# Attention scores from half-array products: three per map, two maps in the two halves of the array's rows

## The chip, the cores and the metric

The kernel runs on one core of a Trainium2 chip. The metric is the time of one execution on the device in microseconds (us). TensorE (PE in the profile) multiplies matrices, VectorE (DVE), ScalarE (ACT) and GpSimd (POOL) work element by element, SyncE (SP) issues the DMAs. PE loads one operand of each product into its array (the weight load, PEld) and streams the columns of the other through it.

## The reference

One encoder layer is applied to two token groups of 1024 and 256 tokens, with model width 1024. It normalises, projects, runs two kinds of attention, projects back, and goes on with an MLP and a gated embedding. What matters here are the scores:

```python
def _diff_attention(q, k, v, lam, slopes):      # mixer A: 4 heads, two softmax maps each
        sc = jnp.einsum('bqhcd,bkhcd->bhcqk', qb, k) * scale
        sc = sc - slopes[None, :, None, None, None] * dist[None, None, None]
        pr = jax.nn.softmax(sc, axis=-1)
        w = pr[:, :, 0] - lam * pr[:, :, 1]
        return jnp.einsum('bhqk,bkhe->bqhe', w, v)

def _gqa_attention(q, k, v):                    # mixer B: 8 query heads, 2 key/value heads
        sc = jnp.einsum('bqngd,bknd->bngqk', qb, k) * scale
        pr = jax.nn.softmax(sc, axis=-1)
        return jnp.einsum('bngqk,bknd->bqngd', pr, v)
```

Each score is a product over a head dimension of 64, in single precision.

## The kernel before, in words

Single precision is reached with two numbers of a shorter format (float32r): a value is split into a high part and a low part, and products of the parts are added up. The queries (`qd`) and keys (`kd`) lie in DRAM with both parts.

Work in the attention is cut into units (`plan_unit`): a block of 256 queries against its group's 1024 keys ("full"; 48 units) or 256 keys ("short"; 12 units). A unit of mixer A is one head with both maps; a unit of mixer B is one of the two heads that share a tile of queries (`c` says which), for both sub-blocks `i` of 128 queries. Each score tile `sc` is 128 queries by up to 1024 keys in PSUM, and there are two buffers of it.

For one tile, `qk` issues products over all 128 rows of the array. The tile `kt` holds the keys' high parts in rows 0 to 63 and the low parts in rows 64 to 127; the tile `qt` holds the queries' high part in both halves of the rows, and beside it the low part in both halves. Two products (high queries, low queries) thus give all four combinations, for each 512 columns:

```python
            for v in range(2):
                for h0 in range(0, sn, 512):
                    PE.matmul(ps[:, h0:h0 + n], shared["q"][:, cc, v, i * P:(i + 1) * P],
                              kt[:, s0 + h0:s0 + h0 + n], start=v == 0, stop=v == 1)
```

A full tile takes four products, a short tile two. Then VectorE reads the tile: for A it adds the distance term, takes the minimum and writes `p` (L555), for B it takes the maximum (L559), after which ScalarE reads the tile once more for the exponential (L567). When the last reader is done the buffer is free for the next tile. GpSimd or VectorE scales the result (L576 to L588), PE transposes it (`tr`, L603), ScalarE and VectorE split the transposes into high and low parts (`ph` L609, `pl` L614), and PE multiplies them with the values (`av`, L627).

These steps are put into numbered rounds: a unit's `qk` stands some rounds ahead of its transposes (`AW` for A, `BW` for B). In each round, products of the remaining projections (`psa`) and of the output projection (`pso`, both L218) are woven in from a generator, as many as `RATIO` times the costs that the parts of the round return. The rounds give the order in which instructions are written down; a scheduler then sets the final order on each engine, with an instruction placed where its operands and buffers are ready by its own reckoning. Each engine carries out its list in that final order.

Of the kernel before, what the change touches and what calls it, by code (L numbers as in the profile page):

```python
# [23 lines left out]
P = 128  # L24
# [4 lines left out]
T = NP_TOK + NS_TOK  # L29
NT = T // P  # L30
# [4 lines left out]
DISTW = 1920  # L35
# [5 lines left out]
def f(ap):  # L41
    return ap.bitcast(F32)
# [3 lines left out]
def encoder_kernel(ctx: ExitStack, tc: tile.TileContext, x, xT, pT, w_in, w_out, w_ff1, w_ff2, w_gate, w_proj,  # L46
# [3 lines left out]
    LEAD = {4: 2000., 5: 2000., 6: 2000.}  # L50
    PRE = 14000
    Y = (2,0,0)
    QM = 0
    AW = (-7, -6, -5, -4)
    BW = (-6, -4)
    AVD = 2
    PHB = 4
    PLB = 4
    PB = 6
    QTB = 3  # L60
# [17 lines left out]
    AOB = 3  # L78
    LDA = 2
    LC = 500.0  # L80
    RATIO = 0.43

    V, S, G, PE = nc.vector, nc.scalar, nc.gpsimd, nc.tensor
    ON_POOL = (0,)
    dma = nc.sync.dma_start
# [20 lines left out]
    qd = [dp.tile([2, P, T], F32, name=f"qd{i}") for i in range(8)]  # L106
    kd = [dp.tile([2, P, T], F32, name=f"kd{i}") for i in range(5)]
# [308 lines left out]
    for (c0, cn) in TCH:  # L416
        ps = pj("psr")
# [13 lines left out]
    pp = pool("pp", space=PSUM, bufs=1, stack=ats)  # L431
# [1 line left out]
    TILES = {  # L433
        "mm": ([P, 2], F32, 4), "ll": ([P, 2], F32, 4), "rl": ([P, 2], F32, 4), "rla": ([P, 2], F32, 4),
        "o": ([P, 256], F32, 3), "osq": ([P, 256], F32, 1), "or": ([P, 256], F32, 1), "pad": ([P, 16], F32, 1),
        "kt": ([P, T], F32R, 3), f"vt{P}": ([P, NT, P], F32R, 1), "ph": ([P, 2, 256], F32R, PHB), "pl": ([P, 2, 256], F32R, PLB),
        "qt": ([P, 2, 2, 256], F32R, QTB), "p": ([P, 1024], F32, PB), "dist": ([P, DISTW], F16, 1),
        f"vt{2 * P}": ([P, NT, 2 * P], F32R, 1), "pq": ([P, 256], F32, 4), "ml": ([P, 2, 256], F32R, 1),
        "snv": ([P, 256], F32, 1), "snu": ([P, 256], F32, 1),
    }  # L440
# [3 lines left out]
    def tl(tag):  # L444
        shape, dt, bufs = TILES[tag]
        return ap.tile(shape, dt, tag=tag, name=tag, bufs=bufs)
# [21 lines left out]

    def load_q(i, t0):
        qt = tl("qt")  # L470
        for dup in range(2):
            if QM:
                dma(f(qt[dup * 64:(dup + 1) * 64]), qd[i][:, :, t0:t0 + 256].rearrange("v (c d) t -> d c v t", d=64))
                continue
            for c in range(2):
                dma(f(qt[dup * 64:(dup + 1) * 64, c]),
                    qd[i][:, c * 64:(c + 1) * 64, t0:t0 + 256].rearrange("v d t -> d v t"))
        return qt

    dst_t = tl("dist")  # L480
# [1 line left out]
    kv = {}  # L482
# [3 lines left out]
    def at(r, ph, fn):  # L486
        rounds[r].append((PH[ph], len(rounds[r]), fn))
# [15 lines left out]
        at(r, "fin", hi)  # L503
        at(r + 1, "fin", lo)

    def plan_unit(kind, idx, t0, c, b, shared):

        is_a = kind == "A"
        s0, sn = SEGS[t0 >= NP_TOK]
        full = sn == NP_TOK  # L510
        nj = sn // 256
        st = {"ws": [None, None], "p": {}}
        if is_a:
            order = [(0, 0), (0, 1), (1, 0), (1, 1)]
            when = [b + q for q in AW] if full else [b - 5, b - 5, b - 4, b - 4]
        else:
            order = [(0, c), (1, c)]
            when = [b + q for q in BW] if full else [b - 4, b - 4]

        def start():  # L520
            if is_a:
                if ("A", idx) not in kv:
                    kv["A", idx] = ([load_k(idx, i) for i in range(2)],
                                    load_v(vad[idx].rearrange("t v d -> t (v d)")))
# [6 lines left out]
            if c == 0:  # L531
                shared["q"] = load_q(idx, t0)

        at(when[0] - 3, "ld", start)

        def qk(i, cc):
            ps = pp.tile([P, 1024], F32, tag="sc", name="sc", bufs=2)
            kt = st["k"][cc] if is_a else st["k"]
            for v in range(2):
                for h0 in range(0, sn, 512):  # L540
                    n = min(512, sn)
                    PE.matmul(ps[:, h0:h0 + n], shared["q"][:, cc, v, i * P:(i + 1) * P],  # L542
                              kt[:, s0 + h0:s0 + h0 + n], start=v == 0, stop=v == 1)
            st["ps", i, cc] = ps
            return sn * 0.844

        def mx(i, cc):
            ps = st["ps", i, cc]
            p = tl("p" if full else "pq")
            st["p"][i, cc] = p  # L550
            if is_a:
                if cc == 0:
                    st["m", i], st["l", i], st["r", i] = (tl(n) for n in ("mm", "ll", "rla"))
                off = DIST0 - (t0 - s0 + i * P)
                V.tensor_tensor_reduce(out=p[:, :sn], in0=ps[:, :sn], in1=dst_t[:, off:off + sn], scale=SLOPES[idx],  # L555
                                       scalar=3.0e38, op0=ALU.add, op1=ALU.min, accum_out=st["m", i][:, cc:cc + 1])
            else:
                st["m", i], st["l", i], st["r", i] = (tl(n) for n in ("mm", "ll", "rl"))
                V.tensor_reduce(out=st["m", i][:, 0:1], in_=ps[:, :sn], axis=AX.X, op=ALU.max, negate=True)  # L559

        def ex(i, cc):
            p = st["p"][i, cc]
            if is_a:
                S.activation(p[:, :sn], p[:, :sn], AF.Exp, scale=-1.0, bias=st["m", i][:, cc:cc + 1],  # L564
                             accum_out=st["l", i][:, cc:cc + 1])
            else:
                S.activation(p[:, :sn], st["ps", i, cc][:, :sn], AF.Exp, scale=1.0, bias=st["m", i][:, 0:1],  # L567
                             accum_out=st["l", i][:, 0:1])

        def cb(i):  # L570
            rl, l = st["r", i], st["l", i]
            if is_a:


                V.reciprocal(rl[:, 1:2], l[:, 1:2])
                G.tensor_scalar(rl[:, 0:1], rl[:, 1:2], l[:, 0:1], neglam, op0=ALU.mult, op1=ALU.mult)  # L576
                p = st["p"][i, 0]
                p1 = st["p"][i, 1]
                if i in ON_POOL and full:
                    G.tensor_scalar(p1[:, :sn], p1[:, :sn], rl[:, 0:1], 1.0, op0=ALU.mult, op1=ALU.mult)  # L580
# [10 lines left out]
        for (i, cc), r in zip(order, when):  # L591
            at(r, "qk", functools.partial(qk, i, cc))
            at(r + 1, "mx", functools.partial(mx, i, cc))
            at(r + 1, "ex", functools.partial(ex, i, cc))
            if not is_a or cc == 1:
                at(r + 2, "cb", functools.partial(cb, i))

        def tr(j2):
            t = pp.tile([P, 2, 256], F32, tag="tr", name="tr", bufs=2)
# [72 lines left out]
            mixed_out(e + 4, idx, t0, lambda: st["o"])  # L672
        else:
            def f1():
                if c == 0:
# [7 lines left out]
            if c == 1:  # L683
                mixed_out(e + 1, idx, t0, lambda: shared["mx"])

    b = 9
    for h in range(4):
        al = [("A", h, t0, 0, {}) for t0 in (0, 256, 1024, 512, 768)]
        bl = []
        for t0 in (0, 256, 512, 768, 1024):  # L690
            sh = {}
            bl += [("B", 4 + h, t0, c, sh) for c in range(2)]
        for kind, idx, t0, c, sh in (bl[0], bl[1], al[0], bl[8], bl[2], bl[3], al[1], bl[9], bl[4], bl[5],
                                     al[2], al[3], bl[6], bl[7], al[4]):
            plan_unit(kind, idx, t0, c, b, sh)
            b += 4 if t0 < NP_TOK else 1


# [173 lines left out]
    while owed > 0:  # L872
        d = next(side)
# [655 lines left out]
```

## Time and profile before

| | |
|---|---|
| median of 3 runs | 1742.87 us (1741.82 to 1745.6) |
| the profiled execution | 1746.48 us, of which the span of its instructions is 1744.7 us |
| PE busy | 1681.1 us, 96% of the span, 9868 products |
| VectorE, ScalarE, GpSimd busy | 67%, 49%, 38% of the span |
| the stretch with scores | 221 to 698 us from the span's start |
| score products (L542) | 576 |

A row of a group reads: line, engine, operation, tile written <- tiles read, rows and columns of the array that are used, shape, count, then busy time in us and mean length in ns, then idle time of the engine ahead of them and what ended it. A row of the timeline reads: start in us, time to the group's end in us, engine and instruction, count. Products are pipelined: the next one starts before the last one's record ends, so a price is read from start to start.

### The profile page before, as it was taken

The page shows a single profiled execution, that of the slowest core. Times are in us where ns is not written, and L with a number is a line of the kernel's source. Part 1 is how long each engine was busy: PE and PEld are TensorE (multiplying, and loading weights), DVE is VectorE, ACT ScalarE, POOL GpSimd, SP SyncE. Part 2 cuts the span into 40 slices and gives each one's busy share as a digit, 9 for nine tenths or more (in the row PEclk, how much of TensorE's full clock was granted, in tenths as well). Part 3 has the DMA queues.
Part 4 walks back from the last instruction along what each step waited for, and adds up shares of the span by engine and source line. Part 5 has one row for each costly group of instructions (what it writes and reads, how often), then busy time and mean ns, then how long its engine had stood idle before and what let it go on. Part 6 is the DMA issues. An engine that isn't in the chain of part 4 may idle for free.

```text
span 1744.7 us, 27438 instructions
## 1 busy us (share of the span) xinstructions
PE 1681.1 (96%) x9868; PEld 1500.5 (86%) x9868; DVE 1172.2 (67%) x2061; ACT 854.7 (49%) x1735; POOL 660.0 (38%) x638
## 2 busy tenths in 40 slices
PE   8899989999989999997999999999999999999997
PEld 8899878888878888777999999998888888888886
DVE  6757458878778778589766666665664865354666
ACT  7523258777767668455333333333433333344554
POOL 1224345756755556335423332320433400001442
PEclk9999999999999999998999999999999999999999
DMA  9723473443874532471533334339665366532111
GB/s 297 236 74 107 146 191 118 116 130 94 223 217 122 144 117 86 140 228 57 179 138 144 132 127 142 140 136 386 230 226 191 120 205 191 183 112 81 41 43 49
DMA packets 198520, 263.47 MB, mean 151 GB/s; under 512 B 14064, under 2 KB 132720, under 8 KB 198384
## 3 DMA queue, kind: packets, MB, share of 16 engines
q1 hardware_dynamic: 198384, 261.72, 46.9%
q8 instruction: 78, 1.28, 0.3%
q14 instruction: 58, 0.48, 0.1%
HBM read 175.16 MB, written 81.27 MB: 147 GB/s over the span
## 4 chain that ended last, share of the span: by engine, by line
PE 81%; DMA 6%; DVE 4%; issue 3%; POOL 2%; ACT 2%; SPq 1%; POOLq 0%; DVEq 0%; ACTq 0%
PE sc L542 6%; PE psa L218 5%; PE av L627 5%; PE psg L149 5%; PE pso L218 5%; PE tr L603 4%; PE psb L218 3%; PE psv L218 2%; PE psp L149 1%; DMA xt<-in_x 1%; DMA xr<-in_xT 1%; DMA vt<-vad 1%; DVE pl L614 1%; PE f__16369 L149 1%; PE f__16711 L149 1%
## 5 line engine op out<-in xcount | busy, mean ns | idle before, releaser
L614 DVE TENSOR_TENSOR pl<-tr,ph 128x512 fp32r<-128x512 f32 x204 | 138.0, 684 | 43.3 <-ACT ph L609 42.5
L1238 ACT ACTIVATE ao<-ar 128x1280 fp32r<-128x1280 f32 x56 | 71.2, 1272 | 191.0 <-PE f__16373 L149 37.9
L542 PE MATMUL sc<-kt,qt 128*128 128x512 f32 (+1 forms) x576 | 154.9, 392 | 8.2 <-issue 3.8
L1240 DVE TENSOR_TENSOR ao<-ar,ao 128x1280 fp32r<-128x1280 f32 x56 | 93.3, 1665 | 103.4 <-ACT ao L1238 103.4
L609 ACT ACTIVATE ph<-tr 128x512 fp32r<-128x512 f32 x204 | 119.8, 595 | 69.9 <-PE tr L603 68.2
L218 PE MATMUL pso<-ow,mt 128*128 128x512 f32 x480 | 121.7, 399 | 7.5 <-DMA mt<-md 5.7
L542 PEld LDWEIGHTS sc<-kt,qt 128*128 128x128 f32 x576 | 101.0, 191 | 26.9 <-issue 4.2
L603 PE MATMUL tr<-ident,p 128*128 128x128 f32 x768 | 115.6, 274 | 4.1 <-DVE pl L614 3.4
L149 PE MATMUL psg<-gw,n 128*128 128x512 f32 (+1 forms) x504 | 115.3, 385 | 0.0
L218 PEld LDWEIGHTS pso<-ow,mt 128*128 128x128 f32 x480 | 88.9, 190 | 25.4 <-DMA mt<-md 6.4
L149 PEld LDWEIGHTS psg<-gw,n 128*128 128x128 f32 x504 | 91.1, 188 | 19.4
L603 PEld LDWEIGHTS tr<-ident,p 128*128 128x128 f32 x768 | 90.5, 141 | 18.4 <-DVE pl L614 5.1
L627 PE MATMUL av<-ph,vt 128*128 128x256 f32 x544 | 102.6, 290 | 1.4 <-DVE zl L740 1.0
L559 DVE TENSOR_REDUCE mm<-sc 128x1 f32<-128x1024 f32 (+1 forms) x80 | 84.1, 1056 | 25.2 <-PE sc L542 24.5
L1027 ACT ACTIVATE w<-w1s 128x512 fp32r<-128x512 f32 x64 | 40.0, 627 | 122.3 <-POOL w1s L1034 6.8
L588 POOL TENSOR_SCALAR p<-p,rl 128x1024 f32<-128x1024 f32 x64 | 72.9, 1141 | 57.5 <-DVE rl L586 52.8
L627 PE MATMUL av<-pl,vt 128*128 128x256 f32 x408 | 93.6, 311 | 0.0
L627 PEld LDWEIGHTS av<-ph,vt 128*128 128x128 f32 x544 | 83.3, 191 | 7.3 <-DVE zl L740 1.9
L567 ACT ACTIVATE p<-sc,mm 128x1024 f32<-128x1024 f32 x64 | 71.4, 1115 | 33.7 <-DVE mm L559 26.8
L555 DVE CUSTOM_DVE_ANT_0 p<-sc,dist 128x1024 f32<-128x1024 f32 x64 | 76.9, 1217 | 5.2 <-PE sc L542 4.2
L564 ACT ACTIVATE p<-p,mm 128x1024 f32<-128x1024 f32 x64 | 73.5, 1150 | 7.7 <-DVE mm L555 7.6
L1413 POOL TENSOR_TENSOR p_l<-pr,p_h 128x256 fp32r<-128x256 f32 x10 | 7.8, 781 | 183.4 <-ACT p_h L1412 183.4
(1508 smaller groups left out, 4786.8 us busy)
## 6 DMA issues: line engine op xcount, KB each, us to landing
ar<-ad SPq DMA_DIRECT2D x56, 640.0 KB, 4.1
w2r<-in_w_ff SPq DMA_DIRECT2D x56, 512.0 KB, 4.5
qt<-qd SPq DMA_DIRECT2D x160, 128.0 KB, 3.2
ad<-q SPq DMA_DIRECT2D x64, 320.0 KB, 2.2
w1r<-in_w_ff SPq DMA_DIRECT2D x32, 512.0 KB, 3.8
ad<-qs SPq DMA_DIRECT2D x48, 320.0 KB, 2.2
md<-ml SPq DMA_DIRECT2D x40, 256.0 KB, 2.5
mt<-md SPq DMA_DIRECT2D x80, 128.0 KB, 3.4
```

The source lines that it names most:

```text
L149: PE.matmul(ps, a, b, start=start and i == 0, stop=stop and i == n - 1)
L218: PE.matmul(ps, a, b, start=i == 0, stop=i == n - 1)
L542: PE.matmul(ps[:, h0:h0 + n], shared["q"][:, cc, v, i * P:(i + 1) * P], kt[:, s0 + h0:s0 + h0 + n], start=v == 0, stop=v == 1)
L555: V.tensor_tensor_reduce(out=p[:, :sn], in0=ps[:, :sn], in1=dst_t[:, off:off + sn], scale=SLOPES[idx], scalar=3.0e38, op0=ALU.add, op1=ALU ...
L559: V.tensor_reduce(out=st["m", i][:, 0:1], in_=ps[:, :sn], axis=AX.X, op=ALU.max, negate=True)
L564: S.activation(p[:, :sn], p[:, :sn], AF.Exp, scale=-1.0, bias=st["m", i][:, cc:cc + 1], accum_out=st["l", i][:, cc:cc + 1])
L588: G.tensor_scalar(p[:, :sn], p[:, :sn], rl[:, 0:1], 1.0, op0=ALU.mult, op1=ALU.mult)
L603: PE.transpose(t[:, jj, i * P:(i + 1) * P], st["ws"][i][:, j * P:(j + 1) * P], ident)
L609: S.activation(ph, st["tr", j2], AF.Copy)
L614: V.tensor_tensor(pl, st["tr", j2], f(st["ph", j2][:]), op=ALU.subtract)
L627: PE.matmul(st["av"][:, :256], x_, y_, start=j2 == 0 and n == 0, stop=j2 == nj - 1 and n == len(pr) - 1)
L1240: V.tensor_tensor(ao[:, 1], a, f(ao[:, 0]), op=ALU.subtract)
```

## The change

The two maps of a head (A), or the two query heads that share keys (B), get their score tiles together. The keys' high parts and low parts are now two tiles, with map 0 (or the first head) in rows 0 to 63 and map 1 (or the second) in rows 64 to 127; for B, where both use the same keys, these are loaded into both halves. The query tile holds each part once. For each tile there are three products over 64 rows, high by high, high by low, low by high; the fourth, low by low, is left out. A full pair takes twelve half-array products where two full tiles took eight products on all rows; a short pair takes six where there were four. The loop writes one for the upper half of the rows and one for the lower by turns, into the two score buffers.

A unit of B is now one sub-block of 128 queries for both heads (`i0`), so its transposes and values run over heads where they ran over sub-blocks, and its output is put together in two halves (`f1`). The number of `qk` calls falls from 160 to 80. The offsets `AW` and `BW` follow from that, `RATIO` rises from 0.43 to 0.46, and there are four `kt` buffers instead of three.

```diff
-    QM = 0
-    AW = (-7, -6, -5, -4)
-    BW = (-6, -4)
+    AW = (-6, -4)
+    BW = -5
...
-    RATIO = 0.43
+    RATIO = 0.46
...
-    def load_k(i, c):
-        kt = tl("kt")
+    def load_k(i, j=None):
+
+        kts = []
         for v in range(2):
-            dma(f(kt[v * 64:(v + 1) * 64, :]), kd[i][v, c * 64:(c + 1) * 64, :])
-        return kt
+            kt = tl("kt")
+            if j is None:
+                dma(f(kt[:]), kd[i][v])
+            else:
+                for dup in range(2):
+                    dma(f(kt[dup * 64:(dup + 1) * 64, :]), kd[i][v, j * 64:(j + 1) * 64, :])
+            kts.append(kt)
+        return kts
...
     def load_q(i, t0):
         qt = tl("qt")
...
+        dma(f(qt[:]), qd[i][:, :, t0:t0 + 256].rearrange("v p t -> p v t"))
         return qt
...
-        def qk(i, cc):
-            ps = pp.tile([P, 1024], F32, tag="sc", name="sc", bufs=2)
-            kt = st["k"][cc] if is_a else st["k"]
-            for v in range(2):
-                for h0 in range(0, sn, 512):
-                    n = min(512, sn)
-                    PE.matmul(ps[:, h0:h0 + n], shared["q"][:, cc, v, i * P:(i + 1) * P],
-                              kt[:, s0 + h0:s0 + h0 + n], start=v == 0, stop=v == 1)
-            st["ps", i, cc] = ps
-            return sn * 0.844
+        def qk(i):
+
+            pss = [pp.tile([P, 1024], F32, tag="sc", name="sc", bufs=2) for _ in range(2)]
+            n = min(512, sn)
+            for h0 in range(0, sn, 512):
+                for m, (vq, vk) in enumerate(((0, 0), (0, 1), (1, 0))):
+                    for cc in range(2):
+                        rows = slice(cc * 64, cc * 64 + 64)
+                        PE.matmul(pss[cc][:, h0:h0 + n], shared["q"][rows, vq, i * P:(i + 1) * P],
+                                  st["k"][vk][rows, s0 + h0:s0 + h0 + n], start=m == 0, stop=m == 2)
+            for cc in range(2):
+                st["ps", i, cc] = pss[cc]
+            return sn * 1.266
...
-                V.reciprocal(rl[:, 0:1], l[:, 0:1])
-                p = st["p"][i, c]
-                G.tensor_scalar(p[:, :sn], p[:, :sn], rl[:, 0:1], 1.0, op0=ALU.mult, op1=ALU.mult)
+                V.reciprocal(rl, l)
+                for cc in range(2):
+                    p = st["p"][i, cc]
+                    G.tensor_scalar(p[:, :sn], p[:, :sn], rl[:, cc:cc + 1], 1.0, op0=ALU.mult, op1=ALU.mult)
+                    st["ws"][cc] = p
+                return
...
-                x_, y_ = slice(c * 64, c * 64 + 64), slice(64 - c * 64, P - c * 64)
                 tm = tl("osq")
-                S.activation(tm[x_], st["av"][y_, :256], AF.Copy)
-                V.tensor_tensor(shared["mx"][x_], st["av"][x_, :256], tm[x_], op=ALU.add)
+                for cc in range(2):
+                    x_, y_ = slice(cc * 64, cc * 64 + 64), slice(64 - cc * 64, P - cc * 64)
+                    w = slice(cc * P, cc * P + P)
+                    S.activation(tm[x_, w], st["av"][y_, w], AF.Copy)
+                    V.tensor_tensor(shared["mx"][x_, i0 * P:i0 * P + P], st["av"][x_, w], tm[x_, w], op=ALU.add)
```

The final order on PE, first near the start of the attention, before the change, where mixer A's first head gets its first scores. `sc` is a score tile, `kt` and `qt` are keys and queries, `tr` the transposes of B's unit ahead of it and `av` its value products; a count stands at a row's end. The first four score products are those of map 0, the next four those of map 1, and the last four of the eight are map 0 of the next sub-block.

```order
L542 MATMUL sc<-kt,qt 128x512 x4
L603 MATMUL tr<-ident,p 128x128 x8
L542 MATMUL sc<-kt,qt 128x512 x8
L627 MATMUL av<-ph,vt_3087 128x256 x2
L627 MATMUL av<-pl,vt_3087 128x256 x2
```

A map's four products stand together. At the same place of the changed program, the first six are those of map 0, in the upper half of the rows (`sc_3228`), and the last six those of map 1, in the lower half (`sc_3229`):

```order
L543 MATMUL sc<-kt,qt 128x512 x6
L610 MATMUL tr<-ident,p 128x128 x4
L634 MATMUL av<-pl,vt_3090 128x256 x2
L634 MATMUL av<-ph,vt_3090 128x256 x2
L610 MATMUL tr<-ident,p 128x128 x4
L634 MATMUL av<-pl,vt_3090 128x256 x2
L543 MATMUL sc<-kt,qt 128x512 x6
```

All six products of the upper half now stand together, then transposes and value products follow, and the six of the lower half come after these. With the tiles' numbers, the first of the two runs and the row ahead of it read (`kt_3164` is the tile of high keys, `kt_3166` that of low keys):

```order
L634 MATMUL av_3248<-ph_3201,vt128_3090 128x256 x2
L543 MATMUL sc_3228<-kt_3164,qt_3170 128x512
L543 MATMUL sc_3228<-kt_3166,qt_3170 128x512
L543 MATMUL sc_3228<-kt_3164,qt_3170 128x512 x2
L543 MATMUL sc_3228<-kt_3166,qt_3170 128x512
L543 MATMUL sc_3228<-kt_3164,qt_3170 128x512
```

One score tile is written in all six, over both of its blocks of 512 keys. A little earlier, at the second pair of B, the two halves stand beside each other in part (`sc_3172` upper, `sc_3173` lower):

```order
L543 MATMUL sc_3172<-kt_3084,qt_3092 128x512
L543 MATMUL sc_3172<-kt_3087,qt_3092 128x512
L543 MATMUL sc_3172<-kt_3084,qt_3092 128x512
L543 MATMUL sc_3173<-kt_3084,qt_3092 128x512
L543 MATMUL sc_3173<-kt_3087,qt_3092 128x512
L543 MATMUL sc_3173<-kt_3084,qt_3092 128x512
L543 MATMUL sc_3172<-kt_3084,qt_3092 128x512
L543 MATMUL sc_3173<-kt_3084,qt_3092 128x512
L543 MATMUL sc_3172<-kt_3087,qt_3092 128x512
L543 MATMUL sc_3173<-kt_3087,qt_3092 128x512
L543 MATMUL sc_3172<-kt_3084,qt_3092 128x512
L543 MATMUL sc_3173<-kt_3084,qt_3092 128x512
```

Three of the upper half stand ahead of three of the lower, and only the last six go by turns, as the loop writes them.

More of the change, by code (lines that the diff above doesn't have):

```diff
@@ L435, in encoder_kernel @@
         "o": ([P, 256], F32, 3), "osq": ([P, 256], F32, 1), "or": ([P, 256], F32, 1), "pad": ([P, 16], F32, 1),
-        "kt": ([P, T], F32R, 3), f"vt{P}": ([P, NT, P], F32R, 1), "ph": ([P, 2, 256], F32R, PHB), "pl": ([P, 2, 256], F32R, PLB),
-        "qt": ([P, 2, 2, 256], F32R, QTB), "p": ([P, 1024], F32, PB), "dist": ([P, DISTW], F16, 1),
+        "kt": ([P, T], F32R, 4), f"vt{P}": ([P, NT, P], F32R, 1), "ph": ([P, 2, 256], F32R, PHB), "pl": ([P, 2, 256], F32R, PLB),
+        "qt": ([P, 2, 256], F32R, QTB), "p": ([P, 1024], F32, PB), "dist": ([P, DISTW], F16, 1),
         f"vt{2 * P}": ([P, NT, 2 * P], F32R, 1), "pq": ([P, 256], F32, 4), "ml": ([P, 2, 256], F32R, 1),
@@ L470, in load_q @@
         qt = tl("qt")
[L471 to L477, printed above, removed]
+        dma(f(qt[:]), qd[i][:, :, t0:t0 + 256].rearrange("v p t -> p v t"))
         return qt
@@ L504, in mixed_out, with plan_unit @@
         at(r + 1, "fin", lo)
-    def plan_unit(kind, idx, t0, c, b, shared):
+    def plan_unit(kind, idx, t0, i0, b, shared):
         is_a = kind == "A"
@@ L513, in plan_unit @@
         if is_a:
-            order = [(0, 0), (0, 1), (1, 0), (1, 1)]
-            when = [b + q for q in AW] if full else [b - 5, b - 5, b - 4, b - 4]
-        else:
-            order = [(0, c), (1, c)]
-            when = [b + q for q in BW] if full else [b - 4, b - 4]
+            when = {i: b + q for i, q in enumerate(AW)}
+        else:
+            when = {i0: b + BW}
         def start():
@@ L522, in start @@
                 if ("A", idx) not in kv:
-                    kv["A", idx] = ([load_k(idx, i) for i in range(2)],
+                    kv["A", idx] = (load_k(idx),
                                     load_v(vad[idx].rearrange("t v d -> t (v d)")))
@@ L530, in start @@
                 st["k"], st["v"] = kv["B", j]
-            if c == 0:
+            if i0 == 0:
                 shared["q"] = load_q(idx, t0)
-        at(when[0] - 3, "ld", start)
-        def qk(i, cc):
-            ps = pp.tile([P, 1024], F32, tag="sc", name="sc", bufs=2)
-            kt = st["k"][cc] if is_a else st["k"]
-            for v in range(2):
-                for h0 in range(0, sn, 512):
-                    n = min(512, sn)
-                    PE.matmul(ps[:, h0:h0 + n], shared["q"][:, cc, v, i * P:(i + 1) * P],
-                              kt[:, s0 + h0:s0 + h0 + n], start=v == 0, stop=v == 1)
-            st["ps", i, cc] = ps
-            return sn * 0.844
+        at(min(when.values()) - 3, "ld", start)
+        def qk(i):
[10 more added lines that the diff above has]
+            return sn * 1.266
         def mx(i, cc):
@@ L557, in mx @@
             else:
-                st["m", i], st["l", i], st["r", i] = (tl(n) for n in ("mm", "ll", "rl"))
-                V.tensor_reduce(out=st["m", i][:, 0:1], in_=ps[:, :sn], axis=AX.X, op=ALU.max, negate=True)
+                if cc == 0:
+                    st["m", i], st["l", i], st["r", i] = (tl(n) for n in ("mm", "ll", "rl"))
+                V.tensor_reduce(out=st["m", i][:, cc:cc + 1], in_=ps[:, :sn], axis=AX.X, op=ALU.max, negate=True)
         def ex(i, cc):
@@ L566, in ex @@
             else:
-                S.activation(p[:, :sn], st["ps", i, cc][:, :sn], AF.Exp, scale=1.0, bias=st["m", i][:, 0:1],
-                             accum_out=st["l", i][:, 0:1])
+                S.activation(p[:, :sn], st["ps", i, cc][:, :sn], AF.Exp, scale=1.0, bias=st["m", i][:, cc:cc + 1],
+                             accum_out=st["l", i][:, cc:cc + 1])
         def cb(i):
@@ L585, in cb @@
             else:
-                V.reciprocal(rl[:, 0:1], l[:, 0:1])
-                p = st["p"][i, c]
-                G.tensor_scalar(p[:, :sn], p[:, :sn], rl[:, 0:1], 1.0, op0=ALU.mult, op1=ALU.mult)
-            st["ws"][i] = p
[L591 to L596, printed above, removed]
+                V.reciprocal(rl, l)
[4 more added lines that the diff above has]
+                return
+            st["ws"][i] = p
+        for i, r in when.items():
+            at(r, "qk", functools.partial(qk, i))
+            for cc in range(2):
+                at(r + 1, "mx", functools.partial(mx, i, cc))
+            for cc in range(2):
+                at(r + 1, "ex", functools.partial(ex, i, cc))
+            at(r + 2, "cb", functools.partial(cb, i))
         def tr(j2):
@@ L674, in f1 @@
             def f1():
-                if c == 0:
+                if i0 == 0:
                     shared["mx"] = tl("o")
-                x_, y_ = slice(c * 64, c * 64 + 64), slice(64 - c * 64, P - c * 64)
                 tm = tl("osq")
-                S.activation(tm[x_], st["av"][y_, :256], AF.Copy)
-                V.tensor_tensor(shared["mx"][x_], st["av"][x_, :256], tm[x_], op=ALU.add)
+                for cc in range(2):
+                    x_, y_ = slice(cc * 64, cc * 64 + 64), slice(64 - cc * 64, P - cc * 64)
+                    w = slice(cc * P, cc * P + P)
+                    S.activation(tm[x_, w], st["av"][y_, w], AF.Copy)
+                    V.tensor_tensor(shared["mx"][x_, i0 * P:i0 * P + P], st["av"][x_, w], tm[x_, w], op=ALU.add)
             at(e, "fin", f1)
-            if c == 1:
+            if i0 == 1:
                 mixed_out(e + 1, idx, t0, lambda: shared["mx"])
@@ L691, in encoder_kernel @@
             sh = {}
-            bl += [("B", 4 + h, t0, c, sh) for c in range(2)]
-        for kind, idx, t0, c, sh in (bl[0], bl[1], al[0], bl[8], bl[2], bl[3], al[1], bl[9], bl[4], bl[5],
+            bl += [("B", 4 + h, t0, i, sh) for i in range(2)]
+        for kind, idx, t0, i, sh in (bl[0], bl[1], al[0], bl[8], bl[2], bl[3], al[1], bl[9], bl[4], bl[5],
                                      al[2], al[3], bl[6], bl[7], al[4]):
-            plan_unit(kind, idx, t0, c, b, sh)
+            plan_unit(kind, idx, t0, i, b, sh)
             b += 4 if t0 < NP_TOK else 1
```

## The prediction

> **What bounds the kernel now.** I read the page's busy shares first, then the stretch of the attention, then the groups of TensorE there, its waits, and last its timeline.
>
> ```profile
> PE 1681.1 (96%) x9868; PEld 1500.5 (86%) x9868; DVE 1172.2 (67%) x2061; ACT 854.7 (49%) x1735; POOL 660.0 (38%) x638
> PE 81%; DMA 6%; DVE 4%; issue 3%; POOL 2%; ACT 2%; SPq 1%; POOLq 0%; DVEq 0%; ACTq 0%
> 215.00:705.00 490.00, 468.35 (x2912) 409.76 (x2911) 381.68 (x692) 348.58 (x726) 300.73 (x355) 0.99 0.49 140
> ```
>
> TensorE (PE) is busy 96% of the span and has 81% of the chain that ended last. The third row is the stretch of the attention (columns: busy time of PE, weight loads, VectorE, ScalarE, GpSimd, then granted clock, DMA share, GB/s). Of its 490 us PE works 468.35, so 21.65 us are idle, and the next engine, VectorE, is busy 78% of it. Time added to PE's queue here adds to the kernel's time, less what the 21.65 us can take up. Who owns them:
>
> ```profile
> PE av L649 <- DVE osq L644: 6.4, 3, 3.0
> PE sc L542 <- issue: 3.8, 1, 3.8
> PE tr L603 <- DVE pl L614: 2.5, 8, 0.8
> PE pso L218 <- ACT ow L800: 1.8, 1, 1.8
> PE sc L542 <- ACT p L567: 1.3, 2, 1.1
> PE sc L542 <- ACT ph L609: 1.2, 1, 1.2
> PE sc L542 <- ACT pq L567: 1.1, 2, 0.8
> ...
> PE sc L542 <- DVE mm L555: 0.7, 2, 0.4
> ```
>
> About half are waits for VectorE or ScalarE, a few of up to 3.0 us. The scores themselves hardly wait.
>
> **What one product costs.** The groups of the scores, in that stretch:
>
> ```profile
> L542 PE MATMUL sc<-kt,qt 128*128 128x512 f32 x512 | 142.4, 404 | 8.1 <-issue 3.8 <-ACT p L567 1.3 <-ACT ph L609 1.2
> L542 PE MATMUL sc<-kt,qt 128*128 128x256 f32 x64 | 14.1, 297 | 0.1
> ```
>
> 512 products of 512 columns and 64 of 256, all on the whole array (128*128). Their means (404 and 297 ns) overlap one another, so the price is taken from start to start in the timeline (start, length, instruction, count):
>
> ```profile
> 433.71 1.09 PE L542 MATMUL sc<-kt,qt 128*128 128x512 f32 x4
> 434.64 0.40 PE L218 MATMUL psa<-xh,wlq 128*128 128x512 f32 x1
> ...
> 435.10 0.60 PE L603 MATMUL tr<-ident,p 128*128 128x128 f32 x4
> 435.46 1.18 PE L542 MATMUL sc<-kt,qt 128*128 128x512 f32 x4
> 436.47 0.39 PE L627 MATMUL av<-ph,vt 128*128 128x256 f32 x2
> ...
> 437.65 0.60 PE L603 MATMUL tr<-ident,pq 128*128 128x128 f32 x4
> ...
> 447.51 0.28 PE L218 MATMUL psa<-xh,whq 128*128 128x256 f32 x1
> ```
>
> Four products of 512 columns take 434.64 - 433.71 = 0.93 us, 0.23 each. Ten of 256 columns lie between 436.47 and 437.65: 1.18 us, 0.12 each. One recorded product of 512 lasts 0.40 us, so its last 0.40 - 0.23 = 0.17 us (I use 0.16, with 256 columns 0.28 - 0.12) run beneath the next one. That tail is the work in flight. Now the scores cost 512 x 0.23 + 64 x 0.12 = 125.4 us of PE's time.
>
> **The change, part by part.** *Products.* Twelve of half the rows replace eight of all rows per pair of score tiles: 64 full pairs give 768 of 512 columns, 16 short ones 96 of 256. If each takes its own slot, as every product in the trace does, that is 256 x 0.23 + 32 x 0.12 = 62.7 us more. If upper and lower half always ran together, it were 384 x 0.23 + 48 x 0.12 = 94.1 us, 31.3 less than now. Which of the two it is hangs on the order. The loop writes upper and lower alternately; the program has them so only at the first pairs. I counted its whole order: the 864 products stand in 155 unbroken runs, 123 of these runs (567 products) hold products of one half alone, mostly six of them, with transposes, value products or projection products between the one half's run and the other's. The two score tiles of a pair come free one after the other, and the scheduler took whichever half could go. A reader holds a tile for over a microsecond:
>
> ```profile
> L559 DVE TENSOR_REDUCE mm<-sc x80: 400/1214/1226, 223.2 to 686.3; 128x1 f32<-128x1024 f32 x64, 128x1 f32<-128x256 f32 x16
> L567 ACT ACTIVATE p<-sc,mm x64: 1099/1116/1132, 224.5 to 688.4; 128x1024 f32<-128x1024 f32 x64
> L555 DVE CUSTOM_DVE_ANT_0 p<-sc,dist x64: 1204/1216/1225, 236.5 to 702.1; 128x1024 f32<-128x1024 f32 x64
> ```
>
> (min/median/max ns.) For mixer A the tiles are 1.2 us apart, for B the maximum and the exponential hold each of them 2.3 us. A product can only share the array with one that stands right beside it: in 89 places one half follows the other, in 620 a half follows itself. Let each product start with its predecessor where that is of the other half and its own half is free: 47 slots of 512 columns and 4 of 256 go, 47 x 0.23 + 4 x 0.12 = 11.3 us. Bounds: 0, if halves never share, and 11.3, which I take. Net +51.4 us.
>
> *Going in and out of half-array work.* 155 runs make 310 changes between the whole array and its halves; before had none. No row of before shows one. The lower bound is nothing: transposes, another kind of work, enter and leave the same queue free of charge. In the rows above four transposes and four score products take 436.47 - 435.10 = 1.37 us; a transpose starts every 0.11 us,
>
> ```profile
> L603 PE MATMUL tr<-ident,p x741: 269/273/422, 232.4 to 705.0; 128*128 128x128 f32 x186
> ```
>
> since four last 0.60 and one 0.273, (0.60 - 0.273) / 3; and 4 x 0.11 + 4 x 0.23 = 1.36. The upper bound is a queue that runs empty and starts again: the tail of 0.16 us, and a weight load that nothing covers. Loads now hide beneath the product ahead:
>
> ```profile
> 433.47 0.40 PE L218 MATMUL psa<-xh,whq 128*128 128x512 f32 x1
> 433.48 0.88 PEld L542 LDWEIGHTS sc<-kt,qt 128*128 128x128 f32 x4
> ```
>
> The first load of the scores starts with the product ahead of them. Uncovered, its price is at most the 0.11 us of a transpose, which moves only 128 columns against a load of as many. So 0 to 0.27 us a change, 0 to 83.7 us. The transposes use all 128 rows as one piece (128*128 in their row), a half-array product does not, so I count it nearer to a queue that runs empty and take the tail alone: 310 x 0.16 = 49.6 us.
>
> On this point the Trainium skill, TensorEngine Tiling (Array Packing), section Key Properties, says that changing the tiling mode, not merely the tile, drains TensorE. It gives no time; by it the term would lie at the tail or above, and by the row of the transposes at nothing. No run here has shown a change of mode yet.
>
> *Waits.* A slower PE gives VectorE and ScalarE more time, so part of the 21.65 us goes. Bounds: -21.65, if all goes, and +9, if the waits for score tiles (1.3 + 1.2 + 1.1 + 0.7 = 4.3 above) triple since a pair now takes both tiles. I take -6, the waits for VectorE's osq.
>
> *Edits at nothing.* The loads of the queries were
>
> ```profile
> qt<-qd SPq DMA_DIRECT2D x160, 128.0 KB, 3.2
> ```
>
> They fall from 160 issues to 40 and move half the bytes; B's keys take four loads where two were. They go ahead on SP's queue, and the DMA share is 0.49 there. One reciprocal of two columns replaces two; the output of B is copied and added in two halves of 128 columns. These lie on VectorE (22% idle) and ScalarE (29% idle); without that cover it were some 40 small copies and 40 small additions on two engines, a few us, inside the bounds above. The ratio at which the projection is woven in rises from 0.43 to 0.46 while the cost put down for scores falls; the work is the same.
>
> *Sum.* The profiled execution took 1746.48 us (1744.7 of span and 1.8 around it): 1746.5 + 51.4 + 49.6 - 6 = 1841.5. The median of the runs lies 3.6 below it: 1838 us.
>
> **The rivals.** *Changes are free.* The transposes speak for it. Without the 49.6: 1788 us.
>
> *Loads come late.* If a change also uncovers a load, 310 x 0.27 = 83.7 replaces 49.6: 1872. If a load waits for the product ahead whenever both use one half, 620 x 0.11 = 68 us come on top of the forecast: 1906. Against it: the row above, where the load starts 0.01 us after the product ahead. The Trainium skill, TensorE: Matmul & The Clock Gate, section "The mechanism", states for small tiles that a weight load overlaps products in flight only when the row groups differ; for whole-array products the trace disagrees, for halves no row here shows it.
>
> *Halves share the array although they stand apart.* This is the faster side: PE would have to start the lower half's products while transposes stand between. All pairs shared would give 1743 - 31 = 1712. It is faster from 62.7 / 0.23 = 273 shared slots of 432 on, if changes cost nothing; the order lets 51 share. Against it: in the timeline the whole-array work between takes all rows, and the products start one after another.
>
> *The change doesn't reach the bound.* No difference, if PE's added 51 us fell into idle time; there are 21.65 us of it.
>
> **How the numbers follow.** Forecast (slots apart, tail paid) 0.45; free changes 0.27; late loads 0.14 (both forms); other slower outcomes 0.06; halves share, faster, 0.06; no difference 0.02. A measurement of this kernel tells about 0.2% (3.5 us) from no change: faster 0.06, same 0.02, slower 0.92. The likeliest alone, with the waits' bounds and sharing from 0 to 11.3, spans 1822 to 1864. The range reaches down past the free changes with more waits gone, 1776, and up past the first of the late loads, with waits added, to 1892. It leaves out the faster side, no difference, the second of the late loads and some of the free changes, 2 in 10.
>
> **What would show it.** In the profile of the changed kernel: the scores' products listed on half the rows, 768 and 96 of them; in a run of six of one half starts 0.23 us apart; in the few alternating runs two starts within 0.23; after the last score product of a run the next product 0.16 later than its slot (0 by the first rival, 0.27 and more by the second); the attention's stretch about 95 us longer and later stages as long as before. Starts of 0.12 us within runs of one half, or a stretch no longer than 490 us, would prove me wrong.

## The result, and the profile after

The changed kernel takes 1832.33 us (median of 4 runs, 1829.28 to 1833.0), the kernel before 1744.23 us (median of 4). The ratio is 1.0492, with a 95% interval of 1.046 to 1.0524: 88 us slower. The forecast was 1838.

The page's busy shares after the change, then the stretch of the attention (same columns as before; 215 to 791 us now ends as far behind the last score product as 215 to 705 did), then the groups of the score products:

```profile
PE 1775.0 (97%) x10156; PEld 1529.0 (84%) x10156; DVE 1181.0 (65%) x2061; ACT 862.4 (47%) x1775; POOL 660.5 (36%) x638
...
215.00:791.00 576.00, 558.91 (x3182) 435.67 (x3180) 389.68 (x686) 354.62 (x759) 298.28 (x354) 0.99 0.33 103
...
L543 PE MATMUL sc<-kt,qt 64*128 64x512 f32 x768 | 198.1, 416 | 8.3 <-issue 4.9 <-ACT p L570 3.4
L543 PE MATMUL sc<-kt,qt 64*128 64x256 f32 x96 | 18.2, 313 | 1.1 <-DVE mm L557 1.1
```

The products stand on 64 rows (64*128), 768 and 96 of them. The attention's stretch grew from 490 to 576 us, by 86; the span grew by 85.6, so the whole loss is there. PE's idle time in the stretch fell from 21.65 to 17.09 us. The waits that are left:

```profile
PE sc L543 <- issue: 4.9, 1, 4.9
PE sc L543 <- ACT p L570: 3.4, 4, 1.6
PE psa L217 <- DVE zl L749: 2.5, 1, 2.5
```

The waits of the sub-norm's product for VectorE's osq (6.4 us before) have nearly gone (0.4). What PE does with the added time, its timeline shows. First a run of one half, six products of the upper or lower rows alone:

```profile
240.50 0.48 PE L634 MATMUL av<-pl,vt 128*128 128x256 f32 x2
240.91 1.65 PE L543 MATMUL sc<-kt,qt 64*128 64x512 f32 x6
242.50 0.39 PE L217 MATMUL psa<-xh,whq 128*128 128x256 f32 x1
242.72 0.28 PE L217 MATMUL psa<-xh,wlq 128*128 128x256 f32 x1
```

Six products take a slot of 0.23 us each, 1.38 in all, yet 242.50 - 240.91 = 1.59 us go by. The product after them has a slot of 0.22 us (242.72 - 242.50) where 0.12 is its price. And the two value products ahead of the run have 0.41 us (240.91 - 240.50), where two such products, also behind transposes, had 0.32 before (438.32 - 438.00):

```profile
438.00 0.48 PE L627 MATMUL av<-pl,vt 128*128 128x256 f32 x2
438.32 0.40 PE L627 MATMUL av<-ph,vt 128*128 128x256 f32 x2
```

So a run costs 0.09 + 0.21 + 0.10 = 0.40 us beyond its slots. The weight loads on the way out:

```profile
242.50 0.19 PEld L217 LDWEIGHTS psa<-xh,whq 128*128 128x128 f32 x1 [0.36 <-issue]
242.60 0.19 PEld L217 LDWEIGHTS psa<-xh,wlq 128*128 128x128 f32 x1
```

The first load after the run starts together with its product, not with the product ahead, as loads did before; PEld sat idle 0.36 us for it.

Second, one of the few runs in which both halves stand beside each other, twelve products and the transposes behind them:

```profile
233.06 1.67 PE L543 MATMUL sc<-kt,qt 64*128 64x512 f32 x12
234.66 0.33 PE L610 MATMUL tr<-ident,p 128*128 128x128 f32 x1
```

Twelve take 1.60 us, hardly more than six of one half. Halves do share the array.

### The profile page after: what moved, and what is told of

Its sections match the earlier page's. It is cut to its first block, busy times and chain, and to the rows that moved or that the text cites. A ratio compares the mean times of both kernels' runs of the same rounds, so it can differ in the third digit from the quotient of the medians.

```text
span 1830.3 us, 27822 instructions
## 1 busy us (share of the span) xinstructions
PE 1775.0 (97%) x10156; PEld 1529.0 (84%) x10156; DVE 1181.0 (65%) x2061; ACT 862.4 (47%) x1775; POOL 660.5 (36%) x638
## 4 chain that ended last, share of the span: by engine, by line
PE 63%; DVE 2%; issue 1%; POOL 1%; DMA 1%; SPq 1%; ACT 1%; DVEq 0%; POOLq 0%; ACTq 0%
PE psg L148 6%; PE sc L543 4%; PE pso L217 3%; PE av L634 3%; PE tr L610 2%; PE psp L148 1%; PE f__16797 L148 1%; PE f__16455 L148 1%; PE f__15415 L148 1%; PE f__15760 L148 1%; PE f__16097 L148 1%; PE f__15066 L148 1%; PE f__15416 L148 1%; PE f__16456 L148 1%; PE f__14706 L148 1%
## 5 line engine op out<-in xcount | busy, mean ns | idle before, releaser
L543 PE MATMUL sc<-kt,qt 64*128 64x512 f32 (+1 forms) x864 | 211.7, 405 | 9.4 <-issue 4.9
L543 PEld LDWEIGHTS sc<-kt,qt 64*128 64x128 f32 x864 | 131.3, 187 | 58.4 <-issue 16.9
L610 PEld LDWEIGHTS tr<-ident,p 128*128 128x128 f32 x768 | 86.6, 141 | 29.8 <-issue 15.6
L634 PE MATMUL av<-ph,vt 128*128 128x256 f32 x544 | 106.9, 297 | 2.5 <-DVE h_sb L853 1.1
```

Of the source, the lines that this page charges most:

```text
L543: PE.matmul(pss[cc][:, h0:h0 + n], shared["q"][rows, vq, i * P:(i + 1) * P], st["k"][vk][rows, s0 + h0:s0 + h0 + n], start=m == 0, stop=m ...
L610: PE.transpose(t[:, jj, i * P:(i + 1) * P], st["ws"][i][:, j * P:(j + 1) * P], ident)
L634: PE.matmul(st["av"][:, :256], x_, y_, start=j2 == 0 and n == 0, stop=j2 == nj - 1 and n == len(pr) - 1)
```

## Experiments: products and changes, each by itself

The theory after the result: the loss is one slot per product, because the halves mostly stand apart, and about 0.37 us per run for going in and out of half-array work. A rival lays all of it on the products, another all of it on the changes. Two kernels made from the one before separate them.

Changes without more products:

```diff
-                    PE.matmul(ps[:, h0:h0 + n], shared["q"][:, cc, v, i * P:(i + 1) * P],
-                              kt[:, s0 + h0:s0 + h0 + n], start=v == 0, stop=v == 1)
+                    PE.matmul(ps[:, h0:h0 + n], shared["q"][0:64, cc, v, i * P:(i + 1) * P],
+                              kt[0:64, s0 + h0:s0 + h0 + n], start=v == 0, stop=v == 1)
```

> The kernel before, with its two score products per block taken over rows 0 to 63 alone; the other half of the contraction (the keys' low parts) is left out. 576 products as before, in 142 runs, none shared. Theory (a run of half-array products costs about 0.37 us whatever it holds): 142 x 0.37 = 52 us, less 5 to 15 us of waits that a slower TensorE swallows: 1780 to 1792 us. Rival (changes of mode are free, the loss is the number of products): 1744 us.

Measured: 1787.17 us against 1745.31 (ratio 1.0247, 1.0219 to 1.0275), 42 us for 142 runs. Two rows of its timeline, a run of four and what follows:

```profile
300.35 1.18 PE L542 MATMUL sc<-kt,qt 64*128 64x512 f32 x4
301.47 0.50 PE L627 MATMUL av<-ph,vt 128*128 128x256 f32 x2
```

Four take 1.12 us where four on the whole array took 0.93: 0.19 more; six in the changed kernel took 0.21 more. The rival without a price for changes falls.

More products without changes:

```diff
-            for v in range(2):
+            for m, v in enumerate((0, 1, 1)):
...
-                              kt[:, s0 + h0:s0 + h0 + n], start=v == 0, stop=v == 1)
+                              kt[:, s0 + h0:s0 + h0 + n], start=m == 0, stop=m == 2)
```

> The kernel before with three whole-array products per block instead of two (the second is repeated, so the scores hold one term twice): 864 products, as many as in the changed kernel, no change of mode. Theory: 62.7 us more of TensorE's time, less 5 to 15 us of waits: 1792 to 1802 us. Rival (the extra products are hidden or cheaper, the loss is all in the changes of mode): about 1744 to 1760 us.

Measured: 1794.02 us (ratio 1.0279, 1.0257 to 1.0302), 49 us for 62.7 us of products. Both terms are real, and they are of like size. Each comes out 11 to 14 us below its price on PE (142 x 0.37 = 52.5 against 42, with an interval of 38 to 48; 62.7 against 49).

## Experiments: what the price hangs on

Is it the number of rows, or the array's mode? And does it go with the runs, or with the products? The first kernel takes 96 rows:

```diff
-                    PE.matmul(ps[:, h0:h0 + n], shared["q"][:, cc, v, i * P:(i + 1) * P],
-                              kt[:, s0 + h0:s0 + h0 + n], start=v == 0, stop=v == 1)
+                    PE.matmul(ps[:, h0:h0 + n], shared["q"][0:96, cc, v, i * P:(i + 1) * P],
+                              kt[0:96, s0 + h0:s0 + h0 + n], start=v == 0, stop=v == 1)
```

> The kernel before with its score products over rows 0 to 95 (the last quarter of the contraction is left out). Such a product is marked for the whole array, so no run changes the array's mode. Theory (the price is that of the change of mode): no change, 1742 to 1747 us. Rival (any product on fewer rows than its neighbours pays): about the 1787 us of the run with 64 rows.

Measured: 1751.9 us (median of 10, 1744.52 to 1753.58) against 1744.46 (ratio 1.0029, 1.0009 to 1.0048). That is 5 us above the expected band, and a sixth of what 64 rows cost. Its profiled execution has a span of 1745.3 us and these score products:

```profile
L542 PE MATMUL sc<-kt,qt 96*128 96x512 f32 x512 | 143.1, 405 | 7.5 <-issue 4.0 <-ACT p L567 1.5 <-ACT pq L567 1.1
```

Before, the same group was busy 142.4 us with a mean of 404 ns. So a product on 96 rows pays nothing that the trace shows; where the 0.3% between the medians comes from stays open, since the ten times lie in two groups, around 1746 and 1753, and the profiled one belongs to the lower.

The second kernel has twice the changes and half the half-array products:

```diff
-            for v in range(2):
-                for h0 in range(0, sn, 512):
-                    n = min(512, sn)
-                    PE.matmul(ps[:, h0:h0 + n], shared["q"][:, cc, v, i * P:(i + 1) * P],
-                              kt[:, s0 + h0:s0 + h0 + n], start=v == 0, stop=v == 1)
+            for h0 in range(0, sn, 512):
+                for v in range(2):
+                    n = min(512, sn)
+                    rows = slice(0, 64 if v == 0 else P)
+                    PE.matmul(ps[:, h0:h0 + n], shared["q"][rows, cc, v, i * P:(i + 1) * P],
+                              kt[rows, s0 + h0:s0 + h0 + n], start=v == 0, stop=v == 1)
```

> The kernel before with only the first of its two products per block over rows 0 to 63 and the second over all rows, by turns (the keys' low parts are left out for the queries' high parts): 288 half-array products in 287 runs, so twice the runs of the kernel with all score products on half the rows, and half its half-array products. Theory (a run costs 0.39 us between whole-array products, whatever it holds): 287 x 0.39 = 112 us, less 13 us of waits: about 1843 us, 1825 to 1855. Rival (a half-array product itself is what costs): half of the 42 us there, about 1766 us.

Measured: 1842.32 us (ratio 1.0562, 1.0547 to 1.0578), 98 us for 287 runs. The groups, and one tile's four products by turns with the product behind them (the row merges all four under the shape of the first; the second and the fourth are on all rows):

```profile
L543 PE MATMUL sc<-kt,qt 128*128 128x512 f32 x256 | 128.8, 504 | 1.5 <-DMA qt<-qd 1.5
L543 PE MATMUL sc<-kt,qt 64*128 64x512 f32 x256 | 128.1, 501 | 3.6 <-issue 1.6 <-ACT p L568 1.4 <-ACT pq L568 0.5
...
300.12 1.78 PE L543 MATMUL sc<-kt,qt 64*128 64x512 f32 x4
301.74 0.64 PE L628 MATMUL av<-ph,vt 128*128 128x256 f32 x4
```

The price goes with the runs. Whole-array products next to half-array ones lengthen as much as these do: both have a mean of some 500 ns instead of 404, 0.10 us more. The four take 301.74 - 300.12 = 1.62 us instead of 0.93: 0.69 more. With 0.10 for a load that nothing covers and 0.09 for the array to run out, three full changes and the load of the first make 3 x 0.19 + 0.10 = 0.67. So one change costs about 0.2 us in two parts, and a run about 0.4, or 0.35 where transposes follow (four of them right behind a run last 0.66 us instead of 0.60, so 0.06 shows where other products pay 0.10).

The Trainium skill, TensorEngine Tiling (Array Packing), section Key Properties, says that changing the tiling mode drains TensorE; these traces agree, and put 0.09 us on the drain and 0.10 on the load behind it.

## Experiments: halves kept together

If halves share where they stand side by side, keeping them so should win back what the order lost. The two score tiles become one with a single buffer, so that both come free at one moment, and each product is tied behind the one before:

```diff
-            pss = [pp.tile([P, 1024], F32, tag="sc", name="sc", bufs=2) for _ in range(2)]
+            pair = pp.tile([P, 2, 1024], F32, tag="sc", name="sc", bufs=1)
+            pss = [pair[:, c] for c in range(2)]
...
-                    for cc in range(2):
+                    for cc in (1, 0):
                         rows = slice(cc * 64, cc * 64 + 64)
-                        PE.matmul(pss[cc][:, h0:h0 + n], shared["q"][rows, vq, i * P:(i + 1) * P],
-                                  st["k"][vk][rows, s0 + h0:s0 + h0 + n], start=m == 0, stop=m == 2)
+                        with tc.issue_after(last.ins) if last else contextlib.nullcontext():
+                            last = PE.matmul(pss[cc][:, h0:h0 + n], shared["q"][rows, vq, i * P:(i + 1) * P],
+                                             st["k"][vk][rows, s0 + h0:s0 + h0 + n], start=m == 0, stop=m == 2)
```

> The two score tiles of a pair are one tile with one buffer, so both halves come free at one moment, and each of the twelve products is tied behind the one before, lower and upper half by turns. The program then has 82 runs of half-array products instead of 155, 78 of them strictly by turns. Theory (halves share the array where they stand beside each other; each run costs about 0.37 us for going in and out, as the changed kernel's starts show): products save 94 us against one slot each instead of 18, runs 82 x 0.37 = 30 us instead of 58, so about 1832 - 76 - 27 = 1729 us, plus new waits for the single buffer, up to 25: 1729 to 1755. Rival (halves hardly share, the loss is one slot per product): 1832 - 27 = 1805 or more.

Two more kernels have the same 82 runs, with the loops over `cc`, `h0` and `m` turned, so that six of one half stand ahead of six of the other, or three ahead of three:

> As the run with turns, with the same 82 runs, but in each run six products of the lower half stand ahead of six of the upper. Theory A (TensorE starts a product of the other half ahead of some that stand before it in the program, as the changed kernel's nine runs of six and six suggest, where about 3.5 of 6 slots were saved): 62 x 2.5 x 0.231 = 36 us slower than by turns. Theory B (strictly in the program's order, one slot saved per run): 62 x 5 x 0.231 + 32 x 0.119 = 75 us slower than by turns. Theory C (halves are two independent queues of any depth): the same as by turns.

> As the runs by turns and in blocks of six, with the same 82 runs, but three products of the lower half, then three of the upper, and so on. Theory (a product goes ahead of up to three waiting products of the other half): the halves share fully, as by turns, 1795 to 1801 us. Rival (sharing falls off with the size of the block): half the way to the blocks of six, about 1808 us; strictly in order: nine slots of twelve, 62 x 3 x 0.231 = 43 us slower than by turns.

Measured: by turns 1798.19 us (ratio 1.0306, 1.0283 to 1.0329), blocks of three 1801.99 (1.0322, 1.0297 to 1.0347), blocks of six 1819.14 (1.0421, 1.0395 to 1.0448). One run of twelve and the product behind it, by turns, in blocks of six, in blocks of three:

```profile
241.79 1.66 PE L546 MATMUL sc<-kt,qt 64*128 64x512 f32 x12
243.38 0.50 PE L637 MATMUL av<-ph,vt 128*128 128x256 f32 x2
```

```profile
243.41 2.24 PE L546 MATMUL sc<-kt,qt 64*128 64x512 f32 x12
245.58 0.51 PE L637 MATMUL av<-ph,vt 128*128 128x256 f32 x2
```

```profile
245.75 1.67 PE L546 MATMUL sc<-kt,qt 64*128 64x512 f32 x12
247.35 0.50 PE L637 MATMUL av<-ph,vt 128*128 128x256 f32 x2
```

By turns twelve take 1.59 us, six slots and a change, so the sharing is full. Blocks of three also take 1.60: sharing is full there too, although the program lists three of one half ahead of the other's first; strictly in that order it would be nine slots and a change, 2.3 us. Blocks of six take 2.17, 0.57 more, or 2.5 slots: 3.5 of 6 are shared. That is theory A on PE; strictly in the program's order it would be 11 slots, 2.7 us. In time it was 21 us instead of 36: by turns PE idles 60.7 us in the stretch, in blocks of six 44.8 (567.00 - 522.25, from 215 to 782 us), so 16 us went into idle time.

But by turns was expected at 1729 to 1755, and came out at 1798. Its stretch of the attention, and its first waits:

```profile
215.00:759.00 544.00, 483.31 (x3193) 393.12 (x3193) 385.91 (x690) 353.85 (x764) 302.87 (x356) 0.96 0.34 108
...
PE tr L613 <- DVE pl L624: 19.8, 20, 3.3
PE sc L546 <- issue: 6.8, 4, 4.5
PE sc L546 <- ACT p L573: 5.7, 9, 1.3
```

PE idles 544.00 - 483.31 = 60.7 us there, against 21.65 before. The granted clock is 0.96, against 0.99 before, so some products also ran slower; I estimate this from the two rows at no more than 0.04 x 544 - 0.01 x 490 = 17 us. I first put that down to too little lead, and moved the scores a round ahead:

```diff
-    AW = (-6, -4)
-    BW = -5
+    AW = (-7, -5)
+    BW = -6
```

> The run by turns, with the scores of both mixers one round earlier (offsets -7 and -5, and -6). Its waits of TensorE (57 us in the stage against 18 before) are put down to bursts on VectorE and to the single buffer. Theory (the waits are for a late reader of the pair, more lead helps): 1765 to 1790 us, still above the kernel before, since shared products and changes of mode together cost as much as the stacked ones. Rival (the burst itself is the limit, lead doesn't help): 1795 to 1805 us.

Measured: 1790.48 us (ratio 1.0262, 1.0247 to 1.0277), 8 us better, and half a us above what the theory allowed. PE still idles 59.5 us in the stretch (536.00 - 476.55, from 215 to 751 us). Lead is not the main thing. The single buffer itself was tried with stacked whole-array products, beside a kernel that has the pair in one round but keeps two buffers:

```diff
-    AW = (-7, -6, -5, -4)
-    BW = (-6, -4)
+    AW = (-6, -6, -4, -4)
+    BW = (-5, -5)
...
-            ps = pp.tile([P, 1024], F32, tag="sc", name="sc", bufs=2)
+            half = cc if is_a else i
+            if half == 0:
+                st["pair"] = pp.tile([P, 2, 1024], F32, tag="sc", name="sc", bufs=1)
+            ps = st["pair"][:, half]
```

> The kernel before, with its stacked whole-array products, but the two score tiles of a pair in one tile with one buffer and issued in the same round, as in the run by turns: 84 runs of mostly eight products. No change of mode, TensorE's work as before. Theory (the run by turns missed its forecast because of the single buffer: 61 us idle in the stage against 22): 30 to 50 us slower than before, 1775 to 1795. Rival (its waits come with half-array products, the single buffer alone costs little): 1744 to 1755.

> The kernel before with both tiles of a pair issued in the same round (offsets -6, -6, -4, -4 and -5, -5), but with two separate buffers as before. Theory (the round is not what matters, the buffers are): 1740 to 1755. Rival (two tiles read in one round make VectorE's bursts and TensorE waits for them): 1765 to 1790.

(The second of them has the offsets alone.) Measured: 1793.9 us with one buffer (ratio 1.0286, 1.0259 to 1.0313), 1743.18 with two (0.9994, 0.9979 to 1.0009). The stretch of the first:

```profile
215.00:757.00 542.00, 488.47 (x2945) 421.82 (x2943) 389.27 (x699) 350.29 (x733) 302.23 (x364) 0.97 0.44 127
...
PE tr L606 <- DVE pl L617: 14.8, 17, 2.2
```

It idles 53.5 us and waits most for the same step as by turns (VectorE's `pl`), with no half-array product in it. So the single buffer costs 50 us, and the round nothing. Of the 50, 32 are idle time (53.5 - 21.65); the granted clock of 0.97 and waits too short for the profile may be the rest, which is not shown. Under one and the same buffer, shared half-array products (1798) are no better than stacked ones (1794): 94.1 us of shared slots and 82 runs at 0.37, 30 us, make 124; the stacked products cost 125.4.

A version with pairs kept together and two buffers for the pair was not tried; it needs twice the room for scores. By the sums above (124 against 125.4 us) I estimate that it would tie with the kernel before, not beat it.

## Why the prediction was right, and where its sizes were off

The direction, the cause and the place hold: the halves stand apart in PE's final order, products take a slot each, going in and out of half-array work costs time, and the attention's stretch grew by 86 us (95 were forecast) while later stages stayed as they were. Inside the sum two steps were wrong, in the sharing and in the changes, and three sizes were off. The terms, with what the trace shows:

- **Products, +62.7 us.** Right. Within a run of one half, starts lie 0.23 us apart, and the kernel with three whole-array products shows the term by itself.
- **Sharing, -11.3 us.** Mis-sized: about -18, counted from the starts in the mixed runs. The step that failed is "let each product start with its predecessor": a product also goes ahead of some of the other half that wait, so six and six share 3.5 slots, not one.
- **Changes, 310 x 0.16 = 49.6 us.** A value between nothing and 0.27 was right, and the size a little low: some 58 us, at 0.40 for each of the 155 runs, or 0.35 for the 70 with transposes behind them. But "take the tail alone" was the wrong mechanism, and its 0.16 comes near the 0.19 by luck. What is paid is 0.09 for the array to run out and 0.10 for an uncovered load; the bound above (0.16 + 0.11) had both parts, with the first too large.
- **Waits, -6 us.** Mis-sized: 62.7 - 18 + 58 = 103 us of added work made 86, so some 17 were swallowed, and 11 to 15 in each of the three kernels that only slow PE (52.5 to 42, 62.7 to 49, 113 to 98). Only 4.6 us are idle time that went (21.65 to 17.09). Some 4 us more are 18 other products that now stand outside the stretch (3182 - 2912 = 270 more in it, where 288 were added; 0.23 us each); 11 of them lie in the 85 us behind it (410 products against 399), which take no longer for it. The rest, some 8 us, would be waits shorter than the 0.16 us by which a recorded product outlasts its slot, which the idle time does not show; that is argued, not shown. One reading of the waits was off too: of the 18.8 us that the prediction lists, 15.0 end at VectorE or ScalarE, not about half.

Two of the three errors, -7 and +8, nearly cancel, which is luck; the third, -11, is what the 9 us come from by which the stretch grew less than forecast, and the median came out 6 us below the forecast. Of the rivals, free changes (1788) fall with the kernel on half rows and the one with twice the changes. A change that also uncovers a load (1872) has the mechanism right, as the loads on the way out show, and the price too high: 0.19 us, not 0.27. Loads that wait for a product of their own half (1906) fall with starts 0.23 us apart inside a run. The Trainium skill, TensorE: Matmul & The Clock Gate, section "The mechanism", says that weight loads overlap products in flight only when the row groups differ; here loads of the same half stay covered within a run, and the measurement decides. That PE's added work falls into idle time is ruled out by the 86 us. Halves that share although whole-array work stands between did not happen: runs of one half kept a slot per product.

## What to carry to other kernels

Half-array products can pay only where both halves stand together in the queue's final order, and where a run is long enough for its 0.4 us (no run here came out faster than the kernel before): check the built order, not the loop. Two things that must meet should come free by one event, but not at the price of a buffer; one score buffer instead of two cost 50 us here, more than the 31 us that full sharing would have saved in products. Count the stalls that a slower engine will swallow, here 11 to 17 us whatever the slowing was.

## What the runs showed of the hardware that was not expected

- TensorE does not keep strictly to the program's order between the two halves of the rows: with three products of one half ahead of three of the other, twelve took 1.60 us, as by turns (1.59); with six ahead of six, 2.17. So PE's list is not carried out strictly in its final order there. The Trainium skill, TensorE: Matmul & The Clock Gate, section "The mechanism", says that products run strictly in the program's order; for two halves these runs differ.
- A change between whole-array and half-array work costs some 0.2 us, about half of it an uncovered weight load. A product on 96 rows shows none of it (mean 405 ns against 404).
- Half-array products of one half are as slow as whole-array ones, 0.23 us for 512 columns; the gain lies in the sharing alone, and there it is full (twelve in six slots).
